# A two-layer decoder trunk on one core: x already transposed by the host and zero products at the beginning, the last sum of squares on VectorE and the last rows stored in three parts

## The chip, the core and the metric

One core of a Trainium2 chip. Its engines run side by side and wait for one another by semaphores: TensorE (PE, with its weight loads PEld), VectorE (DVE), ScalarE (ACT), GpSimd (POOL), and SyncE (SP), which issues transfers. ACT can issue transfers from a queue of its own as well; either kind of issue is worked through by the same 16 DMA engines. The metric is the device time of one execution in microseconds (us); lower is better.

## The reference

The input x is 256 tokens by 1024 features. Two layers, each `h = h + mixer(norm(h))`, then `h = h + ffn(norm(h))`, and a last norm. Only the first mixer and the last norm are touched by the change:

```python
def rmsnorm(x, g, eps=RMS_EPS):
    xf = x.astype(jnp.float32)
    y = xf * lax.rsqrt(jnp.mean(jnp.square(xf), axis=-1, keepdims=True) + eps)
    return (y * g.astype(jnp.float32)).astype(x.dtype)

def moba_mixer(x, w_in, w_out, cos, sin):
    B, S, _ = x.shape
    H, Dh = A_HEADS, A_HEAD_DIM
    qkv = (x @ w_in).reshape(B, S, 3, H, Dh)
    q = apply_rotary(qkv[:, :, 0], cos, sin).transpose(0, 2, 1, 3)
    k = apply_rotary(qkv[:, :, 1], cos, sin).transpose(0, 2, 1, 3)
```

With 256 tokens there is one block, so the first mixer is causal attention with 8 heads; the second is differential attention. The feed-forward part is a gated one of width 2816 with a causal convolution.

## The kernel before

All weights are cut into 98 chunks of 128 x 2048 floats (1.05 MB), which SP loads in the order of their use into three buffers (`raw`). Each chunk is split into a rounded high part (`wh`, a cast on ACT, L166) and the rest (`wl`, a subtraction on DVE, L168), and a product is made in three passes: high by high, high by low, low by high. A buffer of `raw` comes free when DVE has made the `wl` of it; the transfer of the chunk three further on waits for that.

The first mixer begins with V for heads 0 to 3 (chunks 0 and 1), then Q (2 and 3), K (4 and 5), Q and K of heads 4 to 7 (6 to 9) and V of these (10 and 11). For a product, the tokens of x must lie along the free axis: the kernel loads x by rows (tile `h`, four transfers of 128 x 512), transposes it on PE (`gain_t`, L272, 16 blocks of 128 x 128), and writes high and low part into `xx`, multiplied by the norm's gain (ACT L275, DVE L278). The norm's factor of each token (`stats` L235 on ACT, `rstd` L240 on DVE and a power on POOL, L242) enters V when it is evacuated (`evac_v`, L371 on ACT) and Q and K by the table of the rotation (`tables`: two transposes on PE at L347, then two products on DVE, L350). `evac_qk` copies the rotated halves on ACT (`swap`, L362) and makes three DVE instructions (L364 to L366) from them.

From the kernel's start to the end of the first V products the order is written out by hand (`tc.manual_schedule`, with places from `PLAN["first"]`); behind that the framework orders each engine's instructions by its own estimates, and these orders are fixed when the program runs: an engine that waits holds everything behind it. `split_upto` and `PLAN["catch"]` say how far the splits run ahead.

Before the first product PE makes 8 transposes of the identity (L853) and later three more (L861). At the end (`finish`), token tile 1 is added in pieces; `piece` takes the sum of squares on ACT (L647) and multiplies by the gain on DVE (L649); `scaled` takes the power on POOL (L657), scales 640 columns on DVE and 384 on ACT and stores the two parts from SP and from ACT.

## Time and profile before

| | |
|---|---|
| median of three runs | 610.37 us (608.74 to 613.03) |
| the profiled execution | 610.75 us, of which the span of the trace is 608.8 us |
| PE busy | 596.1 us (98% of the span) |
| DVE busy | 446.4 us (73%) |
| ACT busy | 347.0 us (57%) |
| POOL busy | 18.4 us (3%) |

A matmul's duration in the trace includes the time in which its result drains; in a row of back-to-back products the spacing of their starts is what each costs. PE is busy nearly throughout, so the places at which it has nothing to do, or has to do what isn't a product, are few; they lie in the first 11 us, before the first scores, and behind the last product. Transfers count as landed for the instruction that waits for them.

### The profile page before, as it was taken

The page shows a single profiled execution, that of the slowest core. Times are in us where ns is not written, and L with a number is a line of the kernel's source. Part 1 is how long each engine was busy: PE and PEld are TensorE (multiplying, and loading weights), DVE is VectorE, ACT ScalarE, POOL GpSimd, SP SyncE. Part 2 cuts the span into 40 slices and gives each one's busy share as a digit, 9 for nine tenths or more (in the row PEclk, how much of TensorE's full clock was granted, in tenths as well). Part 3 has the DMA queues.
Part 4 walks back from the last instruction along what each step waited for, and adds up shares of the span by engine and source line. Part 5 has one row for each costly group of instructions (what it writes and reads, how often), then busy time and mean ns, then how long its engine had stood idle before and what let it go on. Part 6 is the DMA issues. An engine that isn't in the chain of part 4 may idle for free.

```text
span 608.8 us, 8918 instructions
## 1 busy us (share of the span) xinstructions
PE 596.1 (98%) x3467; PEld 522.7 (86%) x3467; DVE 446.4 (73%) x796; ACT 347.0 (57%) x600; POOL 18.4 (3%) x29
## 2 busy tenths in 40 slices
PE   8999999999999999999999999999999999999995
PEld 6989988888888888888889998888788888888885
DVE  4789684589766677667585899965896776667745
ACT  5867574286455444554577798744754455544422
POOL 1200000000000000000010001011000000000000
PEclk9999999999999999999999999999999999999998
DMA  8676444255556455555353622451745565555101
GB/s 297 219 301 241 153 156 178 100 207 208 208 207 206 159 192 206 190 168 195 138 210 119 226 71 71 158 212 45 267 177 195 192 208 208 207 177 176 64 1 69
DMA packets 16752, 106.20 MB, mean 174 GB/s; under 512 B 2115, under 2 KB 2627, under 8 KB 4422
## 3 DMA queue, kind: packets, MB, share of 16 engines
q1 hardware_dynamic: 16422, 105.24, 47.7%
q8 instruction: 27, 0.44, 0.3%
q10 hardware_dynamic: 288, 0.39, 0.2%
q14 instruction: 15, 0.12, 0.1%
HBM read 104.58 MB, written 1.05 MB: 173 GB/s over the span
## 4 chain that ended last, share of the span: by engine, by line
PE 84%; ACT 5%; DVE 4%; DMA 3%; issue 3%; POOL 0%; SPq 0%; POOLq 0%; ACTq 0%
PE acc L286 43%; PE wk L286 35%; DMA raw<-in_wts_dram 3%; DVE wl L168 2%; PE wk L385 2%; ACT swap L362 2%; ACT wh L166 1%; ACT sc L400 1%; PE wk L426 1%; PE wk L272 1%; PE wk L259 1%; DVE arena L366 0%; DVE swap L365 0%; DVE arena L364 0%; PE wk L482 0%
## 5 line engine op out<-in xcount | busy, mean ns | idle before, releaser
L166 ACT CAST wh<-raw 128x1024 fp32r<-128x1024 f32 (+1 forms) x198 | 200.3, 1040 | 162.1 <-issue 122.8
L168 DVE TENSOR_TENSOR wl<-raw,wh 128x1024 fp32r<-128x1024 f32 (+1 forms) x198 | 239.1, 1223 | 71.2 <-ACT wh L166 45.9
L286 PE MATMUL wk<-xx,wh 128*128 128x512 f32 x640 | 153.7, 391 | 1.0 <-DVE zg L718 0.7
L286 PEld LDWEIGHTS wk<-xx,wh 128*128 128x128 f32 x640 | 118.4, 188 | 25.0 <-PE wk L286 0.8
L286 PE MATMUL acc<-wh,arena 128*128 128x512 f32 x472 | 129.8, 392 | 0.0
L286 PEld LDWEIGHTS acc<-wh,arena 128*128 128x128 f32 x472 | 87.0, 188 | 17.3 <-ACT arena L759 0.6
L286 PEld LDWEIGHTS wk<-xx,wl 128*128 128x128 f32 x640 | 82.8, 191 | 3.6
L286 PE MATMUL wk<-xx,wl 128*128 128x256 f32 x640 | 83.9, 283 | 0.0
L286 PE MATMUL acc<-xx,wh 128*128 128x256 f32 x512 | 75.3, 285 | 0.1
L286 PE MATMUL acc<-wl,arena 128*128 128x512 f32 x236 | 71.9, 393 | 0.0
L286 PEld LDWEIGHTS acc<-xx,wh 128*128 128x128 f32 x512 | 67.0, 191 | 0.7 <-ACT wh L166 0.3
L286 PE MATMUL acc<-wh,xx 128*128 128x512 f32 x192 | 56.6, 407 | 1.1 <-ACT xx L275 1.1
L286 PEld LDWEIGHTS acc<-wl,arena 128*128 128x128 f32 x236 | 44.0, 188 | 9.0
L286 PEld LDWEIGHTS acc<-wh,xx 128*128 128x128 f32 x192 | 35.8, 192 | 8.7 <-ACT xx L275 1.5
L286 PE MATMUL acc<-xx,wl 128*128 128x256 f32 x256 | 43.1, 285 | 0.0
L730 DVE SCALAR_TENSOR_TENSOR qsb<-zg,conv,qsb 128x255 f32<-128x255 f32 (+1 forms) x80 | 36.6, 481 | 0.1
L286 PEld LDWEIGHTS acc<-xx,wl 128*128 128x128 f32 x256 | 35.7, 191 | 0.1
L362 ACT COPY swap<-acc 8x512 f32<-8x512 f32 (+1 forms) x48 | 27.7, 578 | 11.9 <-PE acc L286 9.6
L760 DVE TENSOR_TENSOR arena<-qsb,arena 128x512 fp32r<-128x512 f32 x22 | 15.2, 691 | 25.9 <-ACT arena L759 25.9
L286 PE MATMUL acc<-wl,xx 128*128 128x512 f32 x96 | 30.0, 402 | 0.0
L400 ACT ACTIVATE sc<-sc,smx 128x128 f32<-128x128 f32 (+1 forms) x48 | 21.3, 446 | 5.2 <-DVE smx L395 5.2
L235 ACT ACTIVATE junk<-h 128x512 f32<-128x512 f32 x16 | 10.1, 632 | 20.6 <-DVE h L617 20.5
(111 smaller groups left out, 466.5 us busy)
## 6 DMA issues: line engine op xcount, KB each, us to landing
raw<-in_wts_dram SPq DMA_DIRECT2D x96, 1024.0 KB, 4.8
h<-in_x_dram SPq DMA_DIRECT2D x4, 256.0 KB, 5.2
raw<-in_wts_dram SPq DMA_DIRECT2D x4, 256.0 KB, 4.9
raw<-in_wts_dram SPq DMA_DIRECT2D x2, 512.0 KB, 7.2
out_dram<-hn SPq DMA_DIRECT2D x2, 320.0 KB, 2.4
tab<-in_rope_dram SPq DMA_DIRECT2D x2, 256.0 KB, 5.3
out_dram<-hn ACTq DMA_DIRECT2D x2, 192.0 KB, 2.7
lamv<-in_lams_dram SPq DMA_DIRECT2D x1, 128.0 KB, 7.6
```

Source lines behind the costliest of these rows:

```text
L166: nc.scalar.copy(hi, r)
L168: nc.vector.tensor_tensor(lo, r, hi.bitcast(F32), op=ALU.subtract)
L235: return nc.scalar.activation(junk, h[t][:, cols(i)], AF.Square, scale=1.0 / 32.0, accum_out=st[t][1][:, i:i + 1])
L259: nc.tensor.transpose(p[:, k * 128:(k + 1) * 128], st[t][0][:, (4 * i + k) * 128:(4 * i + k + 1) * 128], ident)
L272: nc.tensor.transpose(p[:, k * 128:(k + 1) * 128], h[t][:, (4 * i + k) * 128:(4 * i + k + 1) * 128], ident)
L286: return lambda: nc.tensor.matmul(o, l() if callable(l) else l, r() if callable(r) else r, start=start, stop=stop)
L362: nc.scalar.copy(w[a:a + half], pv[b:b + half])
L385: nc.tensor.matmul(p[:, b * 128:(b + 1) * 128], q[r, hl, tq * 128:(tq + 1) * 128], k[r, hl, tk * 128:(tk + 1) * 128], start=True, stop=True)
L400: nc.scalar.activation(es[m][:, c], es[m][:, c], AF.Exp, bias=sm[:, 1, i:i + 1], scale=scale, accum_out=sm[:, 2, i:i + 1])
L426: nc.tensor.transpose(p[:, b * 128:(b + 1) * 128], es[0][:, b * 128:(b + 1) * 128], ident)
L730: nc.vector.scalar_tensor_tensor(y[:, b, s:], z[:, :256 - s], cw[:, 2 - s:3 - s], y[:, b, s:], op0=ALU.mult, op1=ALU.add)
L760: nc.vector.tensor_tensor(g[:, 1], y, g[:, 0].bitcast(F32), op=ALU.subtract)
```

## The change

**Beginning.** The host hands x in a transposed layout as well (`xt`, eight blocks k of 128 features x 256 tokens); block 0 comes in one array with the gains (`xgain`). ACT's queue loads `xg` and block 1, SP loads the other blocks in pairs between the pieces of chunks 0 and 1, both now cut into four pieces of 128 x 512. `prep_x` makes the high part of a block from SBUF on ACT (block 0: on DVE) and the low part on DVE, for both token tiles at once. The 16 transposes of x, the transposes at L861 and the places of `PLAN["first"]` are gone. The first V runs block by block: six products of 512 columns for each k. The rows of x (`h`, two transfers of 0.52 MB) come behind chunk 3, followed by one transfer (`small`, 0.48 MB) for rotation table, convolution weights and the other small inputs, which were four transfers.

PE's first instructions are 8 products of 512 columns with a tile of zeros, which DVE writes, in place of 8 transposes of the identity. `stats`, `rstd` and `evac_v` of the first norm come behind the splits of chunks 2 and 3. The gains of the feed-forward norms and of the last norm are replicated over the partitions by the transfer (0.52 MB each) and no longer by POOL from a row of 4 KB.

**End.** The last quarter's sum of squares is one DVE instruction (`tensor_tensor_reduce`), which adds the sum so far as well; the product with the gain is left out for the last 336 columns and made together with the scaling. The last rows are scaled and stored in three parts (352 columns on ACT; 336 and 336 on DVE). Tile 0's second store goes from SP in place of ACT.

```diff
--- before.py
+++ after.py
...
-    "first": (4, 4, 6, 8, 9, 23, 18, 25, 32, 35, 37),
...
-    def load_x(t, i):
-        c = slice(i * 512, (i + 1) * 512)
-        nc.sync.dma_start(h[t][:, c], x[t * 128:(t + 1) * 128, c])
+    def load_h():
+        for t in range(NT):
+            nc.sync.dma_start(h[t], x[t * 128:(t + 1) * 128])
 
     def load_gain(i):
-        row = work.tile([128, D], F32, name="junk", bufs=1)[0:1]
-        nc.sync.dma_start(row, gains[i:i + 1, :])
         g_tiles[i] = work.tile([128, D], F32, name="gain", bufs=1)
-        nc.gpsimd.partition_broadcast(g_tiles[i], row)
-
-    gT = const.tile([128, DEPTH, KT], F32, name="gT")
-    load_x(0, 0)
-    nc.sync.dma_start(gT, gainsT)
+        nc.sync.dma_start(g_tiles[i], bass.AP(tensor=gains.tensor, offset=gains.offset + i * D,
+                                              ap=[[0, 128], [1, D]]))
+
+
+    xg = const.tile([128, DEPTH * KT + S], F32, name="xg")
+    gT = xg[:, :DEPTH * KT].rearrange("p (l k) -> p l k", l=DEPTH)
+    xts = [arena([4, S]) for i in range(2)]
+
+    def x_tile(k):
+        return xts[k // 4][:, k % 4] if k else xg[:, DEPTH * KT:]
+
+    def load_xt(engine, k, n):
+        engine.dma_start(xts[k // 4][:, k % 4:k % 4 + n], xt[:, k:k + n])
+
+    nc.scalar.dma_start(xg, xgain)
+    load_xt(nc.scalar, 1, 1)
+
+    idle = work.tile([128, D], F32, name="junk", bufs=1)[:, :640].bitcast(F32R)
+    nc.vector.memset(idle.bitcast(F32), 0.0)
...
+    small_t = const.tile([128, SMALL], F32, name="small")
+    tab = small_t[:, :2 * S].rearrange("p (i q) -> p i q", i=2)
...
-            if c == 0:
+            if c < 2:
                 for i in range(4):
+                    k = 4 * c + i
+                    if k in (2, 4, 6):
+                        load_xt(nc.sync, k, 2)
                     nc.sync.dma_start(r[:, i * 512:(i + 1) * 512], wts[c, :, i * 512:(i + 1) * 512])
-                    if i == 1:
-                        load_x(1, 0)
-            elif c == 1:
-                for i in range(2):
-                    load_x(i, 1)
-                    nc.sync.dma_start(r[:, i * 1024:(i + 1) * 1024], wts[c, :, i * 1024:(i + 1) * 1024])
             else:
                 nc.sync.dma_start(r, wts[c])
+            if c == 3:
+                load_h()
+                nc.sync.dma_start(small_t, small)
...
-    pieces = [(0, i * 512, 512) for i in range(4)]
-    pieces += [(c, i * 1024, 1024) for c in range(1, n_chunks) for i in range(2)]
+    pieces = [(c, i * 512, 512) for c in range(2) for i in range(4)]
+    pieces += [(c, i * 1024, 1024) for c in range(2, n_chunks) for i in range(2)]
...
+    def prep_x(k, engine=None):
+
+        src, g = x_tile(k), gT[:, 0, k:k + 1]
+        hi, lo = (xx[:, k, i].rearrange("p t q -> p (t q)") for i in range(2))
+        if engine is nc.vector:
+            nc.vector.tensor_scalar(hi, src, g, None, op0=ALU.mult)
+        else:
+            nc.scalar.activation(hi, src, AF.Copy, scale=g)
+        nc.vector.scalar_tensor_tensor(lo, src, g, hi.bitcast(F32), op0=ALU.mult, op1=ALU.subtract)
...
-                main = []
-                for c, k, t in ((0, 0, 0), (0, 2, 0), (0, 0, 1), (0, 2, 1),
-                                (1, 0, 0), (1, 0, 1), (1, 2, 0), (1, 2, 1)):
-                    main += proj_part(ps[t], c, 4 * c, k, t, c == 0 and k == 0, c == 1 and k == 2)
...
+                for k in range(KT):
+                    if k == 0:
+                        prep_x(0, nc.vector)
+                    elif k == 1:
+                        prep_x(1)
+                    elif k % 2 == 0:
+                        prep_x(k)
+                        prep_x(k + 1)
+                    split_next()
+                    for ph in range(3):
+                        for t in range(2):
+                            c = k // 4
+                            f = (k % 4) * 512
+                            nc.tensor.matmul(ps[t], (xh, xl, xh)[ph][:, t, k],
+                                             (WH, WH, WL)[ph][c][:, f:f + 512],
+                                             start=k == 0 and ph == 0, stop=k == KT - 1 and ph == 2)
+                split_upto(6)
                 for t in range(2):
-                    sm += [(f[7], lambda t=t: stats(t, 0)), (f[7], lambda t=t: stats(t, 1)),
-                           (f[8], lambda t=t: rstd(t))]
...
-                run(main, sm)
-                load_small()
-                lam_setup()
+                    stats(t, 0)
+                    stats(t, 1)
+                for t in range(2):
+                    rstd(t)
                 fixed.__exit__(None, None, None)
                 slot = 1
-                load_gain(0)
-                later(evac_v, ps[1], 0, 1)
+                for t in (1, 0):
+                    later(evac_v, ps[t], 0, t)
...
+                if slot == 4 and layer == 0:
+                    load_gain(0)
...
-            if i == 2:
-                nc.vector.tensor_tensor(s[t][:, 4:5], s[t][:, 3:4], s[t][:, 2:3], op=ALU.add)
-
-        def scaled(t, v):
+
+        def power(t, v):
             nc.gpsimd.tensor_tensor(s[t][:, 5:6], v, cm05[:, 0:1], op=ALU.pow)
-            r = s[t][:, 5:6]
-            a, b = slice(0, CUT), slice(CUT, D)
-            nc.vector.tensor_scalar(hg[t][:, a], hg[t][:, a], r, None, op0=ALU.mult)
-            nc.sync.dma_start(out[t * 128:(t + 1) * 128, a], hg[t][:, a])
-            nc.scalar.activation(hg[t][:, b], hg[t][:, b], AF.Copy, scale=r)
-            nc.scalar.dma_start(out[t * 128:(t + 1) * 128, b], hg[t][:, b])
+            return s[t][:, 5:6]
...
         add(1, c[3], q[1])
-        piece(1, c[3], 2)
-        scaled(1, s[1][:, 4:5])
+        junk = work.tile([128, 2, 256], F32, name="zu")[:, 0]
+        nc.vector.tensor_tensor_reduce(junk, h[1][:, c[3]], h[1][:, c[3]], 1.0 / 1024.0, s[1][:, 3:4],
+                                       op0=ALU.mult, op1=ALU.add, accum_out=s[1][:, 4:5])
+        r = power(1, s[1][:, 4:5])
+        e = [slice(0, 352), slice(352, 688), slice(688, 1024)]
+        nc.scalar.activation(hg[1][:, e[0]], hg[1][:, e[0]], AF.Copy, scale=r)
+        nc.vector.tensor_scalar(hg[1][:, e[1]], hg[1][:, e[1]], r, None, op0=ALU.mult)
+        store(nc.sync, 1, e[1])
+        store(nc.scalar, 1, e[0])
+        nc.vector.scalar_tensor_tensor(hg[1][:, e[2]], h[1][:, e[2]], r, g[:, e[2]], op0=ALU.mult, op1=ALU.mult)
+        store(nc.sync, 1, e[2])
...
     for i in range(PRE):
-        nc.tensor.transpose(w[:, :128], ident, ident)
+        nc.tensor.matmul(w, idle[:, :128], idle[:, 128:], start=True, stop=True)
...
-    split_next()
-    gain_t(0, 0, 0, ((0, 1),))
-    gain_t(0, 0, 0, ((2, 3),))
-    split_next()
-    for i in range(PRE2):
-        nc.tensor.transpose(w[:, :128], ident, ident)
```

How the rows of three places moved. Names: `wh_128`, `wh_197`, `wh_256`, `wh_301`, `wh_374`, `wh_430` and `wh_460` are the high parts of chunks 0 to 6 before; after the change these are `wh_136`, `wh_187`, `wh_227`, `wh_253`, `wh_326`, `wh_384` and `wh_414` (the number of a `wl` is one higher). PE's first products, before:

```order
L272 MATMUL wk<-ident,h_70 128x128 [waits DMAHW0_49]
L272 MATMUL wk<-ident,h_70 128x128 x3
L861 MATMUL wk<-ident 128x128 x3
L286 MATMUL acc<-wh_128,xx 128x512 [waits Activation_49]
L286 MATMUL acc<-wh_128,xx 128x512 [waits DVE_49]
L286 MATMUL acc<-wl_129,xx 128x512
L286 MATMUL acc<-wh_128,xx 128x512 [waits Activation_49]
L286 MATMUL acc<-wh_128,xx 128x512 [waits DVE_49]
L286 MATMUL acc<-wl_129,xx 128x512 [waits DVE_49]
L272 MATMUL wk<-ident,h_71 128x128 [waits DMAHW4_49]
L272 MATMUL wk<-ident,h_71 128x128 x3
L286 MATMUL acc<-wh_128,xx 128x512 [waits Activation_49] x2
```

and after:

```order
L890 MATMUL wk<-junk 128x512 [waits DVE_49]
L890 MATMUL wk<-junk 128x512 x7
L555 MATMUL acc<-wh_136,xx 128x512 [waits DVE_49,Activation_49]
L555 MATMUL acc<-wh_136,xx 128x512
L555 MATMUL acc<-wh_136,xx 128x512 [waits DVE_49]
L555 MATMUL acc<-wh_136,xx 128x512
L555 MATMUL acc<-wl_137,xx 128x512 [waits DVE_49]
L555 MATMUL acc<-wl_137,xx 128x512
L555 MATMUL acc<-wh_136,xx 128x512 [waits Activation_49]
L555 MATMUL acc<-wh_136,xx 128x512
L555 MATMUL acc<-wh_136,xx 128x512 [waits DVE_49]
L555 MATMUL acc<-wh_136,xx 128x512
```

The transposes between the products are gone; each set of two products now waits for a piece or a block only.

PE in the first half of Q, at the two transposes for the rotation's table (they wait for POOL's power of token tile 0 and 1), before:

```order
L286 MATMUL acc<-xx,wl_257 128x256
L286 MATMUL acc<-xx,wh_256 128x256 x3
L286 MATMUL acc<-xx,wl_257 128x256 x2
L347 MATMUL wk<-ident,st 128x128 [waits Pool_49] x2
L286 MATMUL acc<-xx,wl_257 128x256 [waits DVE_49]
L286 MATMUL acc<-xx,wl_257 128x256
L286 MATMUL acc<-xx,wh_256 128x256 x4
```

and after:

```order
L303 MATMUL acc<-xx,wh_253 128x256 x4
L303 MATMUL acc<-xx,wl_254 128x256 x2
L303 MATMUL acc<-xx,wh_253 128x256 x4
L363 MATMUL wk<-ident,st 128x128 [waits Pool_49]
L303 MATMUL acc<-xx,wh_227 128x256 x4
L303 MATMUL acc<-xx,wl_228 128x256
L363 MATMUL wk<-ident,st 128x128 [waits Pool_49]
L303 MATMUL acc<-xx,wl_228 128x256 x3
```

The two transposes stood together behind 12 products of chunk 2; now they stand behind all 48 of the first half, five products apart.

ACT behind the first norm, before (`swap` copies evacuate Q's first results):

```order
L166 CAST wh_301<-raw_164 128x1024 [waits DMAHW4_49]
L166 CAST wh_301<-raw_164 128x1024
L166 CAST wh_374<-raw_212 128x1024 [waits DMAHW5_49]
L166 CAST wh_374<-raw_212 128x1024
L166 CAST wh_430<-raw_264 128x1024 [waits DMAHW7_49,DVE_49]
L166 CAST wh_430<-raw_264 128x1024
L362 COPY swap_103<-acc 16x512 [waits PE_49]
L362 COPY swap_103<-acc 16x512
L166 CAST wh_460<-raw_307 128x1024 [waits DMAHW4_49,DVE_49]
```

and after:

```order
L242 ACTIVATE junk,st<-h_71 128x512 [waits Activation_49]
L387 ACTIVATE arena<-acc,st 128x512 [waits PE_49,Pool_49]
L222 ACTIVATE le<-ls 128x2 [waits DVE_49]
L183 CAST wh_326<-raw_219 128x1024 [waits DMAHW2_49]
L183 CAST wh_326<-raw_219 128x1024
L378 COPY swap_110<-acc 16x512 [waits PE_49]
L378 COPY swap_110<-acc 16x512
L378 COPY swap_111<-acc 16x512 [waits PE_49]
L378 COPY swap_111<-acc 16x512
L183 CAST wh_384<-raw_233 128x1024 [waits DMAHW3_49]
L183 CAST wh_384<-raw_233 128x1024
L183 CAST wh_414<-raw_259 128x1024 [waits DMAHW4_49]
L183 CAST wh_414<-raw_259 128x1024
```

The casts of chunk 5 stood ahead of Q's copies and now stand behind all four of them; in PE's order of after, products of chunk 6 (Q of heads 4 to 7) stand between those of chunk 5:

```order
L303 MATMUL acc<-xx,wh_384 128x256 [waits Activation_49]
L303 MATMUL acc<-xx,wh_384 128x256 x5
L303 MATMUL acc<-xx,wh_414 128x256 [waits DVE_49,Activation_49]
L303 MATMUL acc<-xx,wh_414 128x256
L303 MATMUL acc<-xx,wh_414 128x256 [waits DVE_49]
L303 MATMUL acc<-xx,wl_385 128x256 [waits DVE_49]
L303 MATMUL acc<-xx,wl_385 128x256 x3
L303 MATMUL acc<-xx,wh_414 128x256
L303 MATMUL acc<-xx,wh_414 128x256 [waits Activation_49]
```

These were behind all of K before; now K's remaining products are queued behind them.

## Rows read from the trace of the kernel before

**Rows 1.** The page's head and its first line on engines: busy us, share, instructions.

```profile
span 608.8 us, 8918 instructions
...
PE 596.1 (98%) x3467; PEld 522.7 (86%) x3467; DVE 446.4 (73%) x796; ACT 347.0 (57%) x600; POOL 18.4 (3%) x29
```

**Rows 2.** Waits of PE: who waited for whom, total us, times, longest.

```profile
PE wk L385 <- DVE arena L366: 1.8, 1, 1.8
```

**Rows 3.** Timeline, 0 to 30 us: start, us, engine, line, operation, count, [idle before].

```profile
5.56 0.62 ACT L166 CAST wh<-raw 128x512 fp32r<-128x512 f32 x1 [3.34 <-DMA raw<-in_wts_dram]
...
6.49 1.51 PE L286 MATMUL acc<-wh,xx 128*128 128x512 f32 x2 [1.07 <-ACT xx L275]
...
9.09 0.63 PE L286 MATMUL acc<-wl,xx 128*128 128x512 f32 x1
...
9.51 1.06 PE L272 MATMUL wk<-ident,h 128*128 128x128 f32 x4
...
11.05 0.60 PE L272 MATMUL wk<-ident,h 128*128 128x128 f32 x4
...
20.60 0.62 PE L286 MATMUL acc<-wh,xx 128*128 128x512 f32 x2
...
21.05 1.10 PE L286 MATMUL acc<-xx,wh 128*128 128x256 f32 x5
```

**Rows 4.** Stretches: length, busy of five engines, PEclk, DMA share, GB/s.

```profile
0.00:4.00 4.00, 2.04 (x10) 2.04 (x11) 0.00 (x0) 1.49 (x2) 2.52 (x12) 1.00 0.44 102
4.00:6.00 2.00, 1.42 (x7) 1.02 (x5) 0.00 (x0) 0.44 (x1) 0.00 (x0) 1.00 1.00 246
6.00:12.00 6.00, 5.51 (x19) 4.21 (x20) 3.91 (x9) 4.36 (x14) 0.00 (x0) 1.00 1.03 371
12.00:16.00 4.00, 4.00 (x21) 3.34 (x20) 4.00 (x10) 3.15 (x8) 0.00 (x0) 1.00 1.02 431
```

**Rows 5.** Timeline, 0 to 30 us: the first norm, casts, products of 256 columns.

```profile
16.57 0.65 ACT L235 ACTIVATE junk<-h 128x512 f32<-128x512 f32 x1
...
17.34 0.63 ACT L235 ACTIVATE junk<-h 128x512 f32<-128x512 f32 x1
...
22.52 3.89 ACT L166 CAST wh<-raw 128x1024 fp32r<-128x1024 f32 x4
...
24.02 1.12 PE L286 MATMUL acc<-xx,wh 128*128 128x256 f32 x8
...
25.22 0.64 PE L286 MATMUL acc<-xx,wh 128*128 128x256 f32 x4
```

**Rows 6.** Timeline, 29 to 60 us: evacuation of Q and K, first scores.

```profile
30.68 1.18 ACT L362 COPY swap<-acc 16x512 f32<-16x512 f32 x2 [0.83 <-PE acc L286]
...
43.07 0.68 DVE L364 TENSOR_TENSOR arena<-acc,tab 128x512 f32<-128x512 f32 x1
...
46.14 1.60 PE L385 MATMUL wk<-arena 128*128 128x128 f32 x12 [1.81 <-DVE arena L366]
...
49.62 1.22 DVE L168 TENSOR_TENSOR wl<-raw,wh 128x1024 fp32r<-128x1024 f32 x1
...
52.61 0.27 PE L426 MATMUL wk<-ident,sc 128*128 128x128 f32 x1
```

**Rows 7.** Timeline of the end, behind PE's last product.

```profile
602.65 0.42 DVE L643 TENSOR_TENSOR h<-wk,h 128x256 f32<-128x256 f32 x1
...
603.95 0.55 POOL L657 TENSOR_TENSOR fin<-fin,cm 128x1 f32<-128x1 f32 x1 [4.49 <-DVE fin L654]
...
604.53 0.55 DVE L660 TENSOR_SCALAR hn<-hn,fin 128x640 f32<-128x640 f32 x1 [0.67 <-POOL fin L657]
605.18 0.35 ACTq L663 DMA_DIRECT2D out_dram<-hn  x1
```

**Rows 8.** Stretches, columns as in rows 4: layer 1's feed-forward norm, and the last stores.

```profile
415.00:428.00 13.00, 13.00 (x65) 10.57 (x64) 8.37 (x11) 8.01 (x14) 1.86 (x2) 1.00 0.01 2
606.00:607.80 1.80, 0.00 (x0) 0.00 (x0) 0.00 (x0) 0.00 (x0) 0.00 (x0) 0.50 0.72 281
```

More of the change, by code (lines that the diff above doesn't have):

```diff
@@ L66, in tile_trunk @@
     x: bass.AP,
+    xt: bass.AP,
     wts: bass.AP,
     gains: bass.AP,
-    gainsT: bass.AP,
-    conv: bass.AP,
-    lams: bass.AP,
-    subln: bass.AP,
+    xgain: bass.AP,
+    small: bass.AP,
     rope: bass.AP,
@@ L174, in split_upto @@
     def split_upto(n):
-        while state["split"] < min(n + 2, len(pieces)):
+        while state["split"] < min(n + 4, len(pieces)):
             split_next()
@@ L252, in hold @@
     def hold(t, a, v):
-        if t == 1 and state["split"] > 14:
+        if t == 1 and state["split"] > 16:
             behind["act"], behind["dve"] = a, v
@@ L334, in mixer @@
         oT = {}
-        tab = work.tile([128, 2, S], F32, name="tab", bufs=1)
         def load_tab():
@@ L669, in finish @@
         piece(0, c[1], 1)
-        scaled(0, s[0][:, 3:4])
+        r = power(0, s[0][:, 3:4])
+        for e in (slice(0, CUT), slice(CUT, D)):
+            if e.start == 0:
+                nc.vector.tensor_scalar(hg[0][:, e], hg[0][:, e], r, None, op0=ALU.mult)
+            else:
+                nc.scalar.activation(hg[0][:, e], hg[0][:, e], AF.Copy, scale=r)
+            store(nc.sync, 0, e)
         add(1, c[1], po[1, 1])
```

35 lines of the change are left out of this document (15 added, 20 removed).

## The prediction

> **What bounds the kernel now.** I read the page first: PE is busy for 98% of a span of 608.8 us [rows 1], so a change gains only where PE waits, or does what is not a product. Then PE's waits: the longest inside the kernel is 1.8 us, before the first scores, for DVE's evacuation of K [rows 2]. Then the timeline of the beginning. The first product starts at 6.49, behind a cast that began when the first piece of weights had landed, at 5.56; the 48 products of the first V end at 21.05, where Q begins [rows 3]. That is 14.56 us. Two products in a row cost 0.45 us at the end of V (20.60 to 21.05), 0.225 each, but 0.42 each at 9.09 to 9.51 [rows 3]: the column of the granted clock reads 1.00 throughout [rows 4], yet the spacing is that of 1.2 GHz early and of 2.4 GHz later. Four transposes took 1.06 at 9.51 and 0.60 at 11.05 [rows 3], so the level rose at about 11 us; PE had been busy without a pause since 6.49, and before that only in parts. So V is 48 x 0.225 = 10.8, some 1.4 of transposes among them, and about 2.2 for the low level.
>
> **The first product.** Ahead of the first piece of weights 0.532 MB were in the queue before (half of x's tile 0.262, gains 0.008, the piece 0.262), and 0.532 are now (`xg` 0.139, block 1 0.131, the piece 0.262). By the stretches' rates 0.41 MB had moved by 4 us, 0.90 by 6, 3.13 by 12 and 4.85 by 16 [rows 4]; 0.532 is passed at 4.5, and the piece had landed 1.1 later. I keep that curve and that lag. The cast starts at 5.56 again, and the first product at 6.2, since `xx` comes from SBUF ahead of the cast: 0.3 gained. The DMA engines are full from 4 us on, share 1.00 to 1.03 [rows 4]. The Trainium skill ("Trainium Kernel Development and Optimization", Key Constraints) says that transfers issued by SP and by ACT run on the same 16 engines and that a second issuer saves only issue time; that agrees with the full share. If ACT's queue were a path of its own, everything behind it would land 0.6 us earlier and the sum would be 606.7.
>
> **V.** The last of the eight blocks and pieces is 3.15 MB into the stream as before: landed at 13.2; a cast of 0.62 and at most 1.22 for the low part [rows 3, 6] give 15.0. PE is later than that: 6.2 + 10.8 = 17.0 if the high level is there at once; if it rises at 11.1 as before, 4.9 us at the low level lose 2.3, so 19.3. For the products of zeros no row shows whether they help. They start at about 1.5 (0.72 and 0.55 for 640 columns on DVE, as in [rows 7]) and keep PE busy for 8 x 0.42 = 3.4 us, more closely than the transposes before; I take the middle, 18.15, with both ends kept. The Trainium skill ("TensorE: Matmul & The Clock Gate", What's actually happening) says that the low level is the default and that activity lifts it. By that page, zeros being activity, V would end near 17.0, which speaks against the rival of the late clock below; no row shows it yet.
>
> **Q and the first norm.** Q's first half is 48 products of 0.12 ((1.12 - 0.64) / 4, [rows 5]): from 18.15 to 23.9. Then PE's row holds the two transposes for the table; the second waits for the power of tile 1, and 43 products of Q are queued behind it. Chunk 3 is complete at 5.25 MB, 16.9 at 0.43 MB per us [rows 4], landed at 18.0; ACT casts it in 2 x 0.97 [rows 5] to 20.0; two squares of 0.77 with their read-outs [rows 5] to 21.5 (the rows of tile 0 landed at 19.3); one square of tile 1, 22.3; the evacuation of V's tile 0 stands next, waits for its power (22.4) and takes 0.65; the other square, 23.8; sum, hand-overs and the power of 0.55 [rows 7], 24.6. PE is there at 18.15 + 5.76 + 0.1 + 0.6 = 24.6. Both are equal, so an earlier V gains nothing more, a later one loses. The same work stood at 21.05 + 53 x 0.12 + 0.3 = 27.7 before: **2.9 gained** here. The transfer `small` (6.78 MB, landed at 21.6) holds DVE no longer than ACT does.
>
> **K.** 43 products bring PE to 30.0, 18 of chunk 4 to 32.15. On ACT the casts of chunk 5 now stand behind Q's four copies; the last two wait for the end of Q and take 1.18 [rows 6], 31.4, and the first cast ends at 32.4: PE waits 0.2. Chunk 6 stands in the middle of K: its cast ends at 34.35, PE is there at 34.1: 0.25. K's first group is complete 48 products on, 40.1; copies 1.18, DVE 0.68, a low part 1.22, DVE 0.68 [rows 6] put the first scores at 43.95, and PE comes at 43.7: 0.25 in place of the 1.8 of before [rows 2]. In all 2.9 - 0.45 + 1.8 - 0.25 = 4.0 ahead, part of it (18 products, 2.2 us) as work already done beside scores 2.2 earlier than 46.14 [rows 6].
>
> **Behind the scores** DVE is what comes late. From 43.95 it has a low part 1.22, four maxima of some 0.43, three evacuations of 0.68, another low part 1.22, and about 1 of small work and of weighing: 51.1 for the first transposed probabilities. PE has the scores (1.35) and 37 products: 49.75. It waits about 1.2, and the lead shrinks to **2.8**; before, these transposes came at 52.61 [rows 6]. From there the work is the same and I let the lead stand; bounds 1.0 (DVE paces two more heads) and 4.0 (no wait).
>
> **What costs nothing.** The replicated gains are 0.52 MB, 1.2 us of the DMA engines each. In layer 1 the place of this load has a DMA share of 0.01 for 13 us [rows 8], which covers it; without the cover a chunk would land 1.2 later. POOL's replication was beside other work.
>
> **The end.** Before: the last sum at 602.65, 0.42, then square, read-out and a sum, and POOL starts at 603.95 [rows 7]. Now one DVE instruction of the same 256 columns, 0.42 by that row: 603.07 + 0.04 + 0.42, with 0.1 for the hand-over 603.6: **0.35 earlier**. The power ends at 604.2. DVE scales 336 columns (0.55 x 336/640 = 0.29 [rows 7]), then multiplies 336 by two factors (0.5, between 0.42 for 256 and 0.68 for 512 [rows 6, 7]): the last store is issued at 605.05 against 605.18 [rows 7]. It carries a third of the bytes, and the other two are 0.4 to 0.6 earlier; the 0.5 MB took most of 606 to 607.8 [rows 8]. Between 0.13 (the issue alone) and 1.0 (two thirds of the bytes out of the way) I take **0.6**, the 0.35 included.
>
> **Sum.** The profiled execution took 610.75: 608.8 of span and 1.95 around it; the median is 0.4 below. 610.75 - 2.8 - 0.6 = 607.35, so 607.3.
>
> **Rivals.**
> Held less: the stream starts faster, since the gains of 64 bytes a row are gone from it and the rate of 246 GB/s at 4 to 6 us is below the later 371 [rows 4]. Half a MB gained there is 0.75 to 1.2 us on chunk 3 and with it on the whole front; with DVE's wait halved the gain is 2.8 + 1.0 + 0.6, with the end at 0.8: 605.5. Against it: the first piece has as many bytes ahead as before.
> Late clock: zero products do not lift the level, which rises at 11.1 again. V ends at 19.3, 1.1 behind the sum, or DVE's lateness goes on for two more heads at about 1 us: 608.5 to 609.4. For it: DVE's work around the scores is not less than before.
> Slower: chunk 6 stands ahead of most of K in PE's fixed row. I have it landed at 28.9; it is needed from 33.4, and each us beyond is a us. The whole gain is gone when it lands 3.4 + 4.5 later, at 36.8; that needs the stream to run at (9.93 - 4.85) / 20 = 0.25 MB per us from 16 us on, the rate of 4 to 6 us. With 0.9 MB more in front of it than before (x twice) and 2.5 us more still, the time is 613. Against it: 0.43 at 12 to 16 [rows 4].
> No change of note: the waits that come up eat all but the end: 610.
>
> **How the numbers follow.** The forecast, 606 to 608.5, gets 0.5; the faster stream (603.8 to 606) 0.22; late clock or DVE's pace (608.5 to 609.9) 0.18; no change 0.06; slower 0.04. Low 604.4 cuts the faster rival's last part, high 609.8 all but the last two cases: 0.15 is left out. A measurement of this kernel can tell about 1%, 604.3 to 616.5: faster 0.07, same 0.9, slower 0.03.
>
> **What would show it.** The first product near 6.2 and the spacing of 0.225 from about 8.7; Q's first product near 18.2; a wait of PE for POOL at the table's second transpose, at most some tenths; first scores at 44, and a wait of about 1 us for DVE behind them, in place of the 1.8; POOL's last power at 603.6 on the old scale, and stores gone 0.6 earlier. The prediction is wrong if the first weights land before 5 us, if PE waits over 1 us for the power or for chunk 5 or 6, or if DVE is late for more than one head.

## The result and the profile after

| | before | changed |
|---|---|---|
| median (9 runs each, same chip) | 609.48 us (608.2 to 613.03) | 606.0 us (605.25 to 606.37) |
| ratio | | 0.9935, 95% interval 0.9917 to 0.9953 |
| the profiled execution | 610.75 us, span 608.8 | 606.2 us, span 604.4 |

The change makes the kernel 0.65% faster: within 1%, as forecast, 1.3 us below the 607.3 and inside the range. The two profiled executions differ by 4.55 us, the medians by 3.5; it is the 4.55 that is explained below. The executions of the kernel before lie 4.8 us apart, those of the changed one 1.1.

The page's first lines (engine: busy us, share, instructions), which answer to [rows 1]:

```profile
span 604.4 us, 8852 instructions
...
PE 594.5 (98%) x3448; PEld 519.5 (86%) x3448; DVE 444.9 (74%) x793; ACT 345.5 (57%) x591; POOL 13.0 (2%) x26
```

PE is busy 1.6 us less, so of the 4.4 us that the span lost, 2.8 were time in which PE had nothing to do. Its waits (total us, times, longest), which answer to [rows 2]:

```profile
PE wk L890 <- DVE junk L127: 1.6, 1, 1.6
PE wk L401 <- DVE arena L382: 0.9, 1, 0.9
...
PE wk L363 <- POOL st L249: 0.2, 1, 0.2
```

The first is the time before the zeros are there. The wait before the first scores (L401) has gone from 1.8 to 0.9 us. The timeline of the beginning (start, us, engine, line, operation, count, [idle before]), which answers to [rows 3]:

```profile
1.58 3.55 PE L890 MATMUL wk<-junk 128*128 128x512 f32 x8 [1.58 <-DVE junk L127]
...
4.47 0.62 ACT L183 CAST wh<-raw 128x512 fp32r<-128x512 f32 x1 [1.32 <-DMA raw<-in_wts_dram]
...
5.18 1.16 PE L555 MATMUL acc<-wh,xx 128*128 128x512 f32 x4
...
9.97 1.07 PE L555 MATMUL acc<-wh,xx 128*128 128x512 f32 x4
...
16.80 0.74 PE L303 MATMUL acc<-xx,wh 128*128 128x256 f32 x4
...
18.21 2.00 ACT L183 CAST wh<-raw 128x1024 fp32r<-128x1024 f32 x2 [0.52 <-DMA raw<-in_wts_dram]
...
24.62 0.32 PE L363 MATMUL wk<-ident,st 128*128 128x128 f32 x1 [0.16 <-POOL st L249]
```

The first weights are there at 4.47, not 5.56; the first four products take 1.16 us, where a single one still cost 0.42 at 9.09 before [rows 3], so PE is at the 2.4 GHz level from the first product; Q begins at 16.80 instead of 21.05. And then the table's second transpose waits for POOL's power until 24.62, where the prediction had it.

**Where the 4.55 us are.** I read the start of the same PE instruction in both traces. The first transposes of layer 0's feed-forward norm start at 114.30 before and 111.67 after: 2.63 ahead. The transposes in layer 1's gate start at 427.82 and 425.20: still 2.62. PE's last product starts at 602.21 and 598.17: 4.04. From there to the end of the span it is 6.59 and 6.25: 0.34. So 2.6 come from the beginning, 1.4 from between 427 and 445 us, where the prediction had nothing, and 0.35 from the end.

The view of PE's waits that [rows 2] is taken from lists two more for the kernel before, and both lie in that stretch:

```profile
PE wk L286 <- DVE zg L718: 0.7, 1, 0.7
PE wk L286 <- DVE qsb L750: 0.4, 1, 0.4
```

The section on time and profile before, which puts PE's idle places in the first 11 us, before the first scores and behind the last product, leaves these two out.

The stretch behind layer 1's feed-forward norm (length, busy us of PE, PEld, DVE, ACT and POOL, PEclk, DMA share, GB/s), before:

```profile
432.00:440.00 8.00, 6.98 (x39) 5.84 (x38) 6.30 (x13) 6.41 (x10) 0.00 (x0) 1.00 0.78 297
```

and after:

```profile
432.00:440.00 8.00, 8.00 (x46) 6.95 (x46) 7.82 (x17) 7.19 (x11) 0.00 (x0) 1.00 0.55 209
```

Before, PE is without work for 1.02 us between 432 and 440, after it is not. Counted from start to start the two waits cost 1.4, because a product's duration includes its drain: from 434.09 to 439.26 PE's products take 5.17 us, and 3.77 for the same ones after (431.47 to 435.24). And before, POOL has 1.31 us of work at 425.55, which is the replication of the gains. The timeline of before there:

```profile
424.47 4.47 DVE L168 TENSOR_TENSOR wl<-raw,wh 128x1024 fp32r<-128x1024 f32 x3 [0.26 <-ACT wh L166]
...
425.55 1.31 POOL L113 PARTITION_BROADCAST gain<-junk  x1 [5.89 <-issue]
...
435.86 2.09 PE L286 MATMUL wk<-xx,wh 128*128 128x512 f32 x8 [0.66 <-DVE zg L718]
...
439.26 2.08 PE L286 MATMUL wk<-xx,wh 128*128 128x512 f32 x8 [0.36 <-DVE qsb L750]
```

Three subtractions take 4.47 us there; after the change three take 3.49. The view by tile says which way (count: shortest, median, longest ns), before and after:

```profile
L168 DVE TENSOR_TENSOR wl<-raw,wh x3: 1212/1226/2189, 424.5 to 427.7; 128x1024 fp32r<-128x1024 f32 x3
```

```profile
L185 DVE TENSOR_TENSOR wl<-raw,wh x6: 1218/1219/1224, 421.8 to 427.5; 128x1024 fp32r<-128x1024 f32 x6
```

One subtraction beside the replication takes 2.19 us instead of 1.22. With it `raw` comes free later: SP issues the next chunk at 427.83, 0.01 behind the gate's transposes, and at 424.24 after, 0.96 ahead of its own. The cast on ACT that waits for a chunk there, before and after:

```profile
432.69 1.05 ACT L166 CAST wh<-raw 128x1024 fp32r<-128x1024 f32 x1 [2.54 <-DMA raw<-in_wts_dram]
```

```profile
429.03 1.05 ACT L183 CAST wh<-raw 128x1024 fp32r<-128x1024 f32 x1 [1.51 <-DMA raw<-in_wts_dram]
```

It starts 4.87 us behind the gate's transposes before and 3.83 behind them after, 1.04 sooner. On ACT and DVE the evacuations for which PE waits (L718, L750) stand behind this cast and its subtraction.

The kernel before replicates gains at two earlier places as well. There too a subtraction is longer, 2.19 us at 27.01 and 1.77 at 312.63. Behind the second PE has no wait; behind the first the next one is that before the first scores, which doesn't go away without POOL's replication (`b_dmagain`, below: 2.13 us). So only the third is shown to reach PE.

### The profile page after: what moved, and what is told of

It is laid out like the page before. It is cut to its first block, busy times and chain, and to the rows that moved or that the text cites. A ratio compares the mean times of both kernels' runs of the same rounds, so it can differ in the third digit from the quotient of the medians.

```text
span 604.4 us, 8852 instructions
## 1 busy us (share of the span) xinstructions
PE 594.5 (98%) x3448; PEld 519.5 (86%) x3448; DVE 444.9 (74%) x793; ACT 345.5 (57%) x591; POOL 13.0 (2%) x26
## 3 DMA queue, kind: packets, MB, share of 16 engines
HBM read 107.18 MB, written 1.05 MB: 179 GB/s over the span
## 4 chain that ended last, share of the span: by engine, by line
PE 85%; ACT 5%; DVE 4%; DMA 3%; issue 2%; POOL 0%; SPq 0%; POOLq 0%; DVEq 0%; ACTq 0%
PE acc L303 43%; PE wk L303 37%; DMA raw<-in_wts_dram 3%; ACT swap L378 2%; PE wk L401 2%; DVE wl L185 1%; ACT sc L416 1%; ACT wh L183 1%; PE wk L442 1%; PE wk L266 1%; DVE arena L382 1%; DVE swap L381 0%; PE wk L834 0%; PE wk L498 0%; PE wk L279 0%
## 5 line engine op out<-in xcount | busy, mean ns | idle before, releaser
L303 PE MATMUL acc<-wh,xx 128*128 128x512 f32 x160 | 45.7, 399 | 0.0
L767 DVE SCALAR_TENSOR_TENSOR qsb<-zg,small,qsb 128x255 f32<-128x255 f32 (+1 forms) x80 | 36.5, 479 | 0.1
L378 ACT COPY swap<-acc 8x512 f32<-8x512 f32 (+1 forms) x48 | 27.7, 577 | 14.9 <-PE acc L303 10.9
L303 PEld LDWEIGHTS acc<-wh,xx 128*128 128x128 f32 x160 | 29.2, 188 | 5.6
L303 PE MATMUL acc<-wl,xx 128*128 128x512 f32 x80 | 24.3, 397 | 0.0
```

Source lines behind the costliest of these rows:

```text
L303: return lambda: nc.tensor.matmul(o, l() if callable(l) else l, r() if callable(r) else r, start=start, stop=stop)
L378: nc.scalar.copy(w[a:a + half], pv[b:b + half])
L767: nc.vector.scalar_tensor_tensor(y[:, b, s:], z[:, :256 - s], cw[:, 2 - s:3 - s], y[:, b, s:], op0=ALU.mult, op1=ALU.add)
```

## The experiments

Medians of 6 to 12 executions each. The changed kernel was run again beside the first group as the mark: 605.93 us (605.49 to 606.12). `a_oldend`, `a_gap`, `a_memset` and `a_c8` ran on another chip, without a mark of their own; `a_memset`, which turned out to change nothing (605.72 us), is the nearest thing to one there.

> The changed kernel again, as the mark for the runs beside it: 606.0 us, ratio to before 0.993 to 0.995; PE's waits at the start of layer 1's feed-forward part (0.7 and 0.4 us before) stay away.

### POOL's replication and DVE

The changed kernel with POOL's replication put back (`a_pool`), and the kernel before with it taken out alone (`b_dmagain`, the same lines with the signs exchanged):

```diff
     def load_gain(i):
+        row = work.tile([128, D], F32, name="junk", bufs=1)[0:1]
+        nc.sync.dma_start(row, gains[i:i + 1, :])
         g_tiles[i] = work.tile([128, D], F32, name="gain", bufs=1)
-        nc.sync.dma_start(g_tiles[i], bass.AP(tensor=gains.tensor, offset=gains.offset + i * D,
-                                              ap=[[0, 128], [1, D]]))
+        nc.gpsimd.partition_broadcast(g_tiles[i], row)
```

> The changed kernel with the gains again replicated by POOL from a row of 4 KB. Theory (POOL's replication slows DVE while it runs): each wl that DVE makes beside it takes 2.1 to 2.2 us instead of 1.22, the next chunk's transfer is issued 1 us later, and PE again waits 0.7 and 0.4 us between 430 and 437 us; 1.0 to 1.4 us slower than the changed kernel, 607.0 to 607.4. Rival (those waits went because everything comes 2.6 us earlier against the transfers): PE doesn't wait there, and the time is that of the changed kernel within 0.2.

> The kernel before with only the gains replicated by the transfer. Theory (POOL slows DVE): the waits of 0.7 and 0.4 us between 435 and 440 us are gone, 1.0 to 1.4 us faster than before. Rival (shift by the beginning): the waits stay, 0 to 0.2 us. Second rival, the prediction's own: the transfers of 0.52 MB delay a chunk somewhere, up to 1.2 us slower.

Measured: `a_pool` 606.73 us (606.37 to 606.80), 0.80 slower than the mark, whose slowest execution is faster than its fastest. Its timeline in layer 1, and the same replication in layer 0:

```profile
422.25 1.42 POOL L111 PARTITION_BROADCAST gain<-junk  x1 [5.79 <-issue]
...
422.42 2.19 DVE L186 TENSOR_TENSOR wl<-raw,wh 128x1024 fp32r<-128x1024 f32 x1
...
432.50 2.09 PE L304 MATMUL wk<-xx,wh 128*128 128x512 f32 x8 [0.52 <-DVE zg L756]
```

```profile
33.01 8.30 POOL L111 PARTITION_BROADCAST gain<-junk  x1 [8.94 <-DMA junk<-in_gains_dram]
...
34.38 5.75 DVE L186 TENSOR_TENSOR wl<-raw,wh 128x1024 fp32r<-128x1024 f32 x5
```

Where POOL begins 0.17 us ahead of the subtraction, the subtraction takes 2.19 and one of the two waits of PE is back (0.52). In layer 0, where the subtraction ahead of the five (32.65, 1.21 us) is still running when POOL begins, DVE loses nothing (1.15 each) and POOL's instruction shows 8.30 us. From the gate's transposes to the last product it is 173.87 us in `a_pool`, 172.95 in the mark, 174.39 before: 0.92 and 1.44 for the replication at this place. The amount expected, 1.0 to 1.4, was too high for the changed kernel, since the second wait did not come back.

`b_dmagain` took 609.66 us (608.14 to 611.5) against 610.74 (607.67 to 613.57, 23 runs) of before: ratio 0.999, interval 0.9974 to 1.0006, so the time alone tells nothing. Its trace does: the two waits at 435 to 440 us are gone, and PE is busy throughout:

```profile
432.00:440.00 8.00, 8.00 (x50) 7.15 (x49) 6.64 (x14) 6.33 (x10) 0.00 (x0) 1.00 0.83 303
```

Here the beginning is that of before, so the rival (that they went because everything comes earlier) falls. From the gate's transposes to the last product it is 172.92 us, as in the changed kernel, so 0.52 MB in place of 4 KB delayed nothing there. For layer 0 this trace doesn't tell, since the level makes its beginning later than that of before (Q at 21.81, see The zeros; its wait before the first scores is 2.13 us). `a_pool` and the mark do: from the table's second transpose to the feed-forward norm's transposes it is 86.91 us with POOL's replication and 86.96 with the transfer.

The Trainium skill ("SBUF — State Buffer", Who interferes with whom) says that a DVE instruction with two inputs in SBUF contends with a GpSimd instruction that reads SBUF, and that the one issued first holds the port while the other waits. The traces agree, in both directions: the subtraction reads `raw` and `wh`; where POOL began first it lost 0.97 us, and where DVE began first POOL's instruction shows 8.30 us instead of 1.42.

Whether it must be an instruction of POOL that reads was asked with one that only writes:

```diff
+        nc.gpsimd.memset(g_tiles[i], 0.0)
         nc.sync.dma_start(g_tiles[i], bass.AP(tensor=gains.tensor, offset=gains.offset + i * D,
```

> The changed kernel, in which POOL also writes zeros to the tile of the gains (128 x 1024) ahead of each of the three transfers that fill it; no order of PE, DVE or ACT changes. Theory one (any work of POOL in SBUF slows DVE's subtraction beside it): one wl of 2 us or more at each of the three places, PE waits about 0.5 us near 432 us, 606.5 to 606.9, as with POOL's replication. Theory two (it is the replication in particular): wl stays at 1.22, 605.9.

Measured: 605.72 us (605.48 to 606.69), wl 1.22. But it decides nothing: the write needs no row of gains, so POOL made it at 417.85 to 418.80, before DVE's subtractions began at 421.13. That question stays open.

### The end

The changed kernel with the end of before (`a_oldend`), and before with the new end (`b_end`); the edit is the part of the diff headed "End", one way and the other.

> The changed kernel with the end of before. The prediction put the new end at 0.6 us; the two traces give 6.2 and 5.85 us from the end of PE's last product to the end of the span. By the prediction 606.5, by the traces 606.3 (changed kernel 605.9); if the end is worth nothing, 605.9.

> The kernel before with only the end changed. From the prediction: 0.6 us faster (0.13 to 1.0). From the two traces, which give 6.2 and 5.85 us from the end of PE's last product to the end of the span: 0.35 us faster. Nothing ahead of the last product should move.

Measured: `a_oldend` 606.28 us (605.75 to 606.57), 0.35 above the mark and 0.56 above `a_memset`, each with overlapping ranges. `b_end` 609.75 us (607.83 to 610.81), ratio 0.9976, interval 0.9959 to 0.9994, 0.4 to 2.5 us faster: the kernel before scatters too much to tell 0.35 from 0.6 with it. The traces are closer: from the start of PE's last product to the end of the span it is 6.59 us before, 6.45 in `a_oldend` and 6.51 in `b_dmagain`, which have the old end, and 6.25 in the changed kernel, 6.26 in the mark and 6.28 in `b_end`. So the new end is worth 0.2 to 0.35 us. The timeline of the mark's end:

```profile
598.64 0.48 DVE L706 CUSTOM_DVE_ANT_0 zu<-h,fin 128x256 f32<-128x256 f32 x1
599.05 0.08 DVE L706 DVE_READ_ACCUMULATOR2_ANT fin<- 128x1 f32 x1
599.21 0.55 POOL L679 TENSOR_TENSOR fin<-fin,cm 128x1 f32<-128x1 f32 x1 [4.29 <-DVE fin L706]
...
599.79 0.39 DVE L711 TENSOR_SCALAR hn<-hn,fin 128x336 f32<-128x336 f32 x1 [0.66 <-POOL fin L679]
600.10 0.56 DVE L714 SCALAR_TENSOR_TENSOR hn<-h,fin,gain 128x336 f32<-128x336 f32 x1
```

Counted from the start of PE's last product (597.74; before 602.21), POOL starts at 1.47 instead of 1.74 [rows 7]: 0.27 gained. The scaling ends at 2.92 instead of 2.94 (on ACT), so DVE's two pieces, the second of which also multiplies by the gain, use that up again. The stores behind it take 3.34 instead of 3.65. So the end of the span is earlier by what the three stores save; without the 0.27 the scaling would have ended later by as much. No run has one without the other.

### The first weights

`a_spq` issues `xg` and block 1 from SP ahead of the weights; `a_g64` leaves them on ACT's queue and puts one more transfer ahead of the weights, 128 rows of 64 bytes:

```diff
-    nc.scalar.dma_start(xg, xgain)
-    load_xt(nc.scalar, 1, 1)
+    nc.sync.dma_start(xg, xgain)
+    load_xt(nc.sync, 1, 1)
```

```diff
+    gx = const.tile([128, DEPTH * KT], F32, name="gx")
+    nc.sync.dma_start(gx, xgain[:, :DEPTH * KT])
     nc.scalar.dma_start(xg, xgain)
```

> The changed kernel with xg and block 1 issued by SP ahead of the weights, not by ACT's queue. Theory one (the first weights land at 4.5 instead of 5.6 because a second queue lets them go beside x): first cast at 5.4 to 5.7, V ends 0.9 us later, 0 to 0.6 us slower at the end, since POOL's power at 24.6 holds PE. Theory two (they land earlier because the gains of 64 bytes a row are no longer ahead of them): first cast at 4.5 as in the changed kernel, nothing changes.

> The changed kernel with one more transfer on SP ahead of the first weights, the gains as 128 rows of 64 bytes (8 KB, which nothing reads). Theory two (rows of 64 bytes cost the queue far more than their bytes): first cast 0.7 to 1.1 us later, 5.2 to 5.6. Theory one (the second queue): 0.1 us later. In both the end moves by 0 to 0.6 us.

Measured: `a_spq` 607.77 us (607.3 to 609.22) and `a_g64` 607.75 (606.62 to 608.78), both 1.8 above the mark. In `a_spq` SP's first issues, the first cast and the table's second transpose are:

```profile
0.74 0.37 SPq L123 DMA_DIRECT2D xg<-in_xgain_dram  x1
1.16 0.42 SPq L121 DMA_DIRECT2D arena<-in_xt_dram  x1
1.63 0.90 SPq L156 DMA_DIRECT2D raw<-in_wts_dram  x2
...
5.07 0.62 ACT L183 CAST wh<-raw 128x512 fp32r<-128x512 f32 x1 [2.83 <-DMA raw<-in_wts_dram]
...
25.80 0.32 PE L363 MATMUL wk<-ident,st 128*128 128x128 f32 x1 [0.17 <-POOL st L249]
```

and in `a_g64`:

```profile
1.17 0.90 SPq L158 DMA_DIRECT2D raw<-in_wts_dram  x2
...
5.41 0.62 ACT L185 CAST wh<-raw 128x512 fp32r<-128x512 f32 x1 [2.25 <-DMA raw<-in_wts_dram]
```

Each issue on SP takes about 0.43 us, one behind the other. In the mark the first weights are issued at 0.73 and cast at 4.56; in `a_spq` at 1.63 and 5.07, before at 1.63 and 5.56. Of the 1.0 us by which the first weights come earlier than before, 0.51 is SP's time for two issues, which ACT's queue took over; the other half remains in `a_spq`, whose weights are issued at the same moment as before. The rows of 64 bytes, put ahead of the weights, cost 0.44 us of issue and 0.41 more for the first cast. So neither theory holds alone. A transfer of 8 KB in long rows was not run, so it isn't shown that the 0.41 is due to the shape of the rows rather than to one transfer more. What neither had: the whole stream is later by as much or more (chunk 3 is cast at 17.94 in the mark, 19.38 and 19.23 in these), the power with it (second transpose at 24.35, 25.80, 25.65), and so nothing is hidden at 24.6; the 0 to 0.6 us expected became 1.8. By 8 us 1.86 MB had moved in the mark, 1.50 and 1.46 in these, and why both move less between 4 and 6 us (266 and 270 GB/s, against 373) and between 6 and 8 (220 and 203, against 355) is open.

### The zeros

Three kernels: the changed one with its products of zeros cut to 128 columns (`a_gap`), with transposes of the identity in their place (`a_ident`), and the kernel before with zeros in place of its transposes of the identity (`b_zero`, 5 and 3 products).

```diff
-        nc.tensor.matmul(w, idle[:, :128], idle[:, 128:], start=True, stop=True)
+        nc.tensor.matmul(w[:, :128], idle[:, :128], idle[:, 128:256], start=True, stop=True)
```

> The changed kernel with its 8 products of zeros cut from 512 to 128 columns: no engine's order changes (in the run with the identity it did, behind the first mixer), and PE has nothing to do from about 2.6 us to the first product at 5.2. Theory (a pause before the first product leaves the level to chance, the rest is held by POOL's power at 24.6): V ends up to 2 us later, the second transpose of the table stays at 24.3 to 24.9, and the median is 605.9 to 606.4; the spread between executions over 1 us (0.6 with 512 columns). Rival (what V loses goes through to the end): 607 to 608. Second rival (the level doesn't depend on the zeros): all as in the changed kernel.

> The changed kernel with the 8 transposes of the identity in place of the 8 products of zeros: PE has nothing to do from about 3.6 us to the first product at 5.2. Theory (the zeros keep PE busy without a pause up to the first product, so the high level is there at once; without them it comes at a moment that differs from execution to execution, 8.7 to 12 us): V ends 1 to 2.3 us later, 17.8 to 19.1; but the second transpose of the table waits for POOL's power at 24.6 in any case, so of that only 0 to 1.0 us reach the end: 606.0 to 607.0, with a spread of over 1.5 us between executions (0.6 for the changed kernel). Rival one (nothing holds PE at 24.6): the full 1 to 2.3 us, 607 to 608.3. Rival two (zeros don't lift the level): V ends at 16.8 as with zeros, and nothing changes.

> The kernel before with products of zeros alone: 5 of 512 columns in place of its first 8 transposes, 3 in place of the later three, so that PE is busy from 1.6 to 5.8 us but for the time in which it waits for x. Theory (the spread of 6 us of the kernel before comes from the moment at which the level rises): spacing of 0.225 from the first product on, V ends at 20.2 or earlier (21.05, 21.8 and 20.2 in three traces), 1 to 2 us faster than before in the median and a spread below 2.5 us. Rival (the spread comes from the transfers of x and of the gains): first weights between 5.5 and 6.0 us, spread and median as before within 0.5.

Measured: `a_gap` 606.46 us (605.92 to 607.03), 0.53 above the mark and 0.74 above `a_memset`. Its timeline of PE:

```profile
1.58 1.97 PE L890 MATMUL wk<-junk 128*128 128x128 f32 x8 [1.58 <-DVE junk L127]
5.30 2.07 PE L555 MATMUL acc<-wh,xx 128*128 128x512 f32 x4 [1.75 <-ACT wh L183]
...
9.73 0.70 PE L555 MATMUL acc<-wl,xx 128*128 128x512 f32 x2
...
18.45 1.00 PE L303 MATMUL acc<-xx,wh 128*128 128x256 f32 x7
...
24.90 0.27 PE L363 MATMUL wk<-ident,st 128*128 128x128 f32 x1
```

PE pauses for 1.75 us before the first product, and the products run at the spacing of 1.2 GHz until about 9.7. V ends 1.82 us later than in the mark (18.45, 16.63), the second transpose stands only 0.55 later (24.90, 24.35), without a wait now. So the zeros buy 1.8 us at the end of V and half a us at the end of the kernel. What holds the rest is less the power than the prediction said. PE's waits in the first half of Q in the mark:

```profile
17.48 0.61 PE L303 MATMUL acc<-xx,wh 128*128 128x256 f32 x3 [0.20 <-ACT wh L183]
...
18.93 0.51 PE L303 MATMUL acc<-xx,wl 128*128 128x256 f32 x2 [0.23 <-DVE wl L185]
...
24.35 0.32 PE L363 MATMUL wk<-ident,st 128*128 128x128 f32 x1
```

From start to start PE loses 0.95 us around the first two, where it waits for the cast and the low part of chunk 2, and 0.3 ahead of the table's second transpose, where it waits for the power. In `a_gap`, 1.82 later, it loses nothing at any of the three. So of the 1.82 us, 0.95 go to chunk 2 and 0.3 to the power.

`a_ident` took 607.6 us (605.41 to 608.39), 1.7 above the mark, but as a whole it isn't the test it was meant to be: the framework ordered the first mixer otherwise. Its V can be read: PE pauses for 1.67 us before the first product, four products take 2.07 us as in `a_gap`, and Q begins at 18.46. Up to the first transposed probabilities it is as early as the mark (50.64, 50.77), at the feed-forward norm 2.0 us behind (113.31, 111.31).

`b_zero` took 609.6 us (608.91 to 610.99) against 610.99 (608.67 to 613.59, 24 runs) of before: 1.4 lower in the median, but the interval of the ratio, 0.9961 to 1.0001, includes no change; the spread is 2.1 us instead of 4.9 (`b_end` and `b_dmagain`, with 12 executions as well: 3.0 and 3.4). Its theory wasn't met: Q begins at 22.35 in its trace, later than in any other. Its granted clock shows 0.69 between 8 and 12 us: the zeros end at 6.2, the first weights are cast at 6.52 instead of 5.56, PE has no product until 7.46, and the level fell once more (one product 0.40 at 8.52, four transposes 1.05 at 10.15).

The level is also one source of the scatter of the kernel before. PE in `b_end` and in `b_dmagain`, whose beginnings are that of before:

```profile
9.05 0.60 PE L272 MATMUL wk<-ident,h 128*128 128x128 f32 x4
...
20.17 1.08 PE L286 MATMUL acc<-xx,wh 128*128 128x256 f32 x5
```

```profile
9.62 1.05 PE L271 MATMUL wk<-ident,h 128*128 128x128 f32 x4
...
11.32 1.05 PE L271 MATMUL wk<-ident,h 128*128 128x128 f32 x4
...
21.81 1.08 PE L285 MATMUL acc<-xx,wh 128*128 128x256 f32 x5
```

Four transposes take 0.60 us (2.4 GHz) at 9.05 in the one, 1.05 (1.2 GHz) still at 11.32 in the other, whose granted clock shows 0.50 between 10 and 12 us; the profiled execution of before stood between [rows 3]. Q begins at 20.17, 21.81 and 21.05, with the same instructions of PE in the same order; counted from the first product, 13.55, 14.88 and 14.56 us later. In the changed kernel, and in `a_pool`, `a_oldend` and `a_memset`, which have its beginning, PE goes from the zeros into the products with no pause, and executions lie 0.4 to 1.2 us apart. That the level makes the whole spread isn't shown: `a_c8` has the same beginning and a spread of 2.8, `a_gap` has the pause and 1.1. Nor is the level always high from the first product on in these: the first four take 1.16 us in the changed kernel and 1.41 in the mark, but 1.97 in `a_pool` and 1.87 in `a_oldend`, where the level rises in the course of them. In `a_spq` and `a_g64`, with the zeros and pauses of 0.37 and 0.90 us behind them, they take 1.22 and 1.21.

### The wait before the first scores

Chunk 8's transfer in two halves, so that the low part that stands ahead of DVE's last evacuation comes earlier:

```diff
+            elif c == 8:
+                for i in range(2):
+                    nc.sync.dma_start(r[:, i * 1024:(i + 1) * 1024], wts[c, :, i * 1024:(i + 1) * 1024])
```

> The changed kernel with the transfer of chunk 8 cut into two halves, so that its first cast, behind which DVE's last evacuation ahead of the first scores stands, can begin earlier; the orders of PE, DVE and ACT change around the scores. If the wait of 0.8 us at the first scores is a loss by itself: 605.0 to 605.3. If DVE paces the first heads anyway, as the prediction has it: 605.7 to 606.2, with a new wait of PE at the first transposed probabilities.

Measured: 607.2 us (605.79 to 608.56), 1.3 above the mark. The first half is cast at 41.12 instead of 41.95, but in the framework's new order the wait before the scores is 1.4 us, not 0.8. So it isn't shown what the wait of 0.9 is worth by itself.

## Why the prediction was right, and where it was wrong

The median of 606.0 lies on the border between the forecast's band (606 to 608.5) and that of the faster stream (603.8 to 606), so the number doesn't choose between the two; what follows goes by the traces.

**What bounds the kernel** held: 98% of the span is PE, and every term sits where PE waits or its clock is low. The list of these places was not complete: of PE's waits before, the prediction took up the longest, and the two of 0.7 and 0.4 us in layer 1 are in the same view.

**The first product** was wrong: cast at 4.47, not 5.56. I counted the bytes ahead of the first weights and not the issues: before, the weights were SP's third transfer, now they are its first. That fired the condition "before 5 us", and the rival of the faster stream (0.22), argued there from the gains of 64 bytes, is part of the result: in `a_spq` and `a_g64`, undoing the new issue and putting short rows ahead each cost 1.3 to 1.45 us at the table's second transpose and 1.8 in the median.

**V** ended at the early end of the bounds (17.0; measured 16.80), not in the middle, which I took (18.15): the level is high from the first product. The rule of the Trainium skill ("TensorE: Matmul & The Clock Gate", What's actually happening) gave this end, if zeros are activity, and the trace agrees with it. `a_gap` shows that it hangs on the zeros: with shorter ones and a pause of 1.75 us V ends at 18.45. That 16.80 is so near 17.0 is luck in part: the first product came at 5.18 instead of 6.2, and V took 11.6 us from there, not 10.8, since PE waits for pieces and blocks in its first third.

**Q and the first norm** came out at 24.62 for 24.6, and for two reasons that cancel. That an earlier V gains little is real (`a_gap`: 1.82 lost in V, 0.55 behind the power), but most of it is held by chunk 2, for which the prediction had no wait (0.95 us in the mark), and only 0.3 by the power. And I had chunk 3 landed at 18.0 with the stream of before, and with one queue it is cast at 19.38: the lag of 1.1 us behind the bytes was too short, and the stream was really faster (4.98 MB by 16 us against 4.85). Landing and cap are one chain, so what delays the stream isn't hidden by the cap.

**K and the scores**: K's first group at 40.1 was exact (the copies start at 40.10). The rows from there, of the changed kernel:

```profile
42.28 2.00 ACT L183 CAST wh<-raw 128x1024 fp32r<-128x1024 f32 x2 [1.00 <-DMA raw<-in_wts_dram]
...
43.36 1.22 DVE L185 TENSOR_TENSOR wl<-raw,wh 128x1024 fp32r<-128x1024 f32 x1 [0.77 <-ACT wh L183]
...
44.51 0.68 DVE L382 TENSOR_TENSOR arena<-arena,swap 48x512 f32<-48x512 f32 x1
...
45.24 1.61 PE L401 MATMUL wk<-arena 128*128 128x128 f32 x12 [0.90 <-DVE arena L382]
...
51.12 0.27 PE L442 MATMUL wk<-ident,sc 128*128 128x128 f32 x1
```

The low part that I had between DVE's evacuations is of chunk 8, and its transfer had not landed: scores at 45.24 instead of 43.95, with a wait of 0.9 instead of 0.25. The wait of 1.2 behind them did not come (0.2 is left): with the scores 1.3 later DVE was no longer late. The first transposed probabilities start at 51.12, predicted 51.1, and the lead kept from there is 2.6, predicted 2.8. Three sums of the prediction are off by 0.1 to 0.2 as they stand: 27.7 less 24.6 is 3.1, not 2.9; the rows behind 40.1 lead to 43.86, not 43.95; and 51.1 less 49.75 is a wait of 1.35, not 1.2.

**What costs nothing** is the step that failed. "POOL's replication was beside other work" looked at POOL's time alone, and put at nothing what it does to DVE. It lay on DVE's path by 0.97 us, through `raw` on a chunk's transfer, and through that on PE: 1.4 us in the pair of traces. It is more than the whole difference between the sum (607.35) and the profiled execution (606.2); 0.2 at the beginning and 0.25 at the end went the other way. That the transfers of 0.52 MB cost nothing held (layer 1 in `b_dmagain`, layer 0 in `a_pool` against the mark).

**The end** was mis-sized: 0.2 to 0.35 for 0.6. POOL starts 0.27 earlier (0.35 predicted), since DVE's sum takes 0.48 + 0.08 for 0.42; scaling takes 0.39 for 0.29 and 0.56 for 0.5; the stores give 0.3.

**The chances**: of the rivals, late clock, no change and slower did not happen. The sum of the prediction with its failed step alone put right, 610.75 - 2.8 - 1.4 - 0.6 = 605.95, is 0.25 from the profiled execution of the changed kernel; without it, the sum was 1.15 off. That the total came out near was luck in part, since the missing 1.4 and the two terms that were too large have opposite signs.

## What to carry to other kernels

Read all of PE's waits and not the longest alone, and before calling an instruction "beside other work", look for what it slows there: here the view by tile, with its shortest and longest time, shows 1.21 and 2.19 us for the same subtraction, and the longest one stands beside POOL. At a kernel's start count the issues ahead of a transfer, at 0.43 us each on one queue, as well as its bytes. And take a second profile of the kernel before if its beginning depends on TensorE's level: three executions of the same instructions began Q at 20.17, 21.05 and 21.81.

## What was not expected of the hardware

- POOL's replication of 128 x 1024 and DVE's subtraction of 128 x 1024 with both inputs in SBUF don't run side by side: 2.19 us instead of 1.22 for DVE where POOL began first, 8.30 instead of 1.42 for POOL where DVE was first.
- Products of zeros count as work for TensorE's level: in the changed kernel they start 0.43 us apart at first, the last one takes 0.40 us instead of 0.63, and the first real products have the spacing of 2.4 GHz; where they ended early and PE paused for 1.75 us (`a_gap`), it was that of 1.2 GHz until about 9.7 us.
- One more transfer ahead of the first weights, 8 KB in rows of 64 bytes, which nothing reads, delayed the first weights by 0.85 us and the fourth chunk by 1.3.
